# One shared credit for the side work of a two-layer trunk kernel, and a different opening

## The chip, the cores and the metric

The kernel runs on one core of a Trainium2 chip. The metric is the device time of one execution in microseconds (us), the median of several runs. The engines are TensorE (PE in the tables, with its weight loads as PEld), VectorE (DVE), ScalarE (ACT), GpSimd (POOL, almost idle here) and SyncE (SP), whose instruction queue issues most of the DMAs.

## The reference, cut to what matters

Two layers; T = 256 tokens, D = 2048, all in float32.

```python
h   = rms_norm(x, g_pre_mix)
z   = h @ w_in          # one projection, columns split among three head groups
o_h = hgrn2(q, f, i, g) # 6 heads, gated linear recurrence in chunks of 64 tokens
o_s = s5(u)             # 512 channels, 2048 complex diagonal states, scan over T, GELU, half-GLU
o_r = retention(q, k, v, g)  # 6 heads, rotary q/k, chunks of 64 tokens, RMSNorm per head
x   = x + rms_norm((concat(o_h, o_s, o_r) * beta) @ w_out, g_post_mix)
x   = x + rms_norm(conv_gated_ffn(rms_norm(x, g_pre_ffn)), g_post_ffn)   # d_ff = 5632
```

## The kernel before, in words

**Chunks.** All weights pass through one list, `chunks`. A chunk is 128 x 2048 float32 (128 x 1536 for a 384-wide group), moved by SP into one of three `raw` buffers (`dma`, L363). Each chunk is split in two halves: ACT casts a half to the high part `whi` (`split_hi`, L400), and DVE subtracts to give the low part `wlo` (`split_lo` through the helper `tt`, L138). `whi` and `wlo` have four buffers each, so that the halves of two chunks can lie ahead of PE. PE multiplies high by high, high by low and low by high: L424 to L426 where the weights are the stationary operand, L430 to L432 where h is, L437 and L442 where two of the three products are merged into one 512-column matmul.

**The order of the chunks** in a layer (201 of them; the second layer begins with chunk 201): 0 to 3 the input of S5, 4 to 27 the projections that feed HGRN2's and retention's gates, queries and keys (384 wide; 36 matmuls of 256 columns each), 28 to 51 those with h stationary (values and output gates; 24 matmuls of 512 columns), 52 to 59 the first part of `w_out` (merged; 16 matmuls of 512 and 16 of 256 columns), 60 the half-GLU of S5, which needs the end of the scan, 61 to 68 the rest of `w_out`, and then the FFN.

**The side work.** The recurrences are Python generators. HGRN2 (`hg_gen`), retention (`rt_gen`) and the gated outputs stand in the list `side`, called the heads below; S5 (`prep`, `s5_pre`, `s5_gen`) stands in `side5`, called the scan. Each `yield` hands back an estimate of the work issued, in ns. After every chunk the main loop (L1411 to L1426) gives each list a credit of its own, so that a chunk is followed by some 2400 of heads and some 2000 of scan:

```python
for lst, b0, b1 in ((side, 2400, 2400), (side5, 2000, 2200)):
    credit = (b1 if ch.last else b0) + min(0, lst.credit)
```

A generator whose input isn't there yet yields 0 and the list is left. HGRN2's first half can begin after chunk 7, its heads proper after chunk 12, retention after chunk 27. The scan's work per quarter `i` is four reads of PE products into `k` tiles, ten 1024-column products and sums on DVE (L138, `k<-k,k`), four pairs of scans of 256 columns (L705, L707) with three short carry chains of eight 4-column products (L138, `s5p`), and eight matmuls for its output. `head_out` is the end of a head group: products (L747), squares (ACT, L753), a reciprocal root in some ten 6-column steps on DVE (`rsqrt_wide`; tiles `rq`, `hrs`), and a scaling (ACT, L768); `gate_out` transposes (PE, L777) and multiplies (DVE, L141).

**The scheduler.** The program is a list of instructions per engine, in an order that follows issue order and data. Each engine works off its own list in order, so what stands ahead of a `wlo` on DVE delays it.

**The opening.** SP issues the constants, the norm gains (`pks`), then the eight tiles of x (L1337) and the first three chunks in turn; chunk 0 comes in two DMAs. `first_pre` (L1281) transposes x (L1288), and `tile` writes the high part of h on ACT (L247) and the low part on DVE (L251). `feed(-1)` has the first chunk's halves cast whole. `warm` (L222) issues matmuls whose result nobody reads.

Of the kernel before, what the change touches and what calls it, by code (L numbers as in the profile page):

```python
# [9 lines left out]
F32 = mybir.dt.float32  # L10
# [5 lines left out]
MULT, ADD, SUB = ALU.mult, ALU.add, ALU.subtract  # L16

P = 128
T = 256
D = 2048  # L20
# [53 lines left out]
def trunk_kernel(ctx, tc, x, w_in, w_out, w_glu, w_up, w_down, pk, s5bc, cst, glast, out, depth=2):  # L74
    nc = tc.nc
    V, S, PE, G = nc.vector, nc.scalar, nc.tensor, nc.gpsimd
# [19 lines left out]
    def nm(s):  # L96
        cnt[0] += 1
        return f"{s}{cnt[0]}"

    def k4(dt=F32):  # L100
        return kp.tile([P, 1024], dt, tag="k", name=nm("k"))

    def spt():
        return sp.tile([P, 512], F32, tag="sp", name=nm("sp"))
# [9 lines left out]
    ones = const.tile([P, P], F32, name="ones")  # L114
    invd = const.tile([P, 1], F32, name="invd")
# [21 lines left out]
    def tt(out, a, b, op):  # L137
        return V.tensor_tensor(out, a, b, op=op)  # L138
# [83 lines left out]
    def warm(n, lhs, rhs):  # L222

        if n:
            ps = spt()
            m = lhs.shape[-1]
            for _ in range(n):
                PE.matmul(ps[0:m, 0:T], lhsT=lhs, rhs=rhs, start=True, stop=True)

    def pair(t, k):  # L230

# [3 lines left out]
    class Norm:  # L235
# [15 lines left out]
            return V.scalar_tensor_tensor(lo, src, PC(self.l, self.gn, k, k + 1), hi.bitcast(F32), op0=MULT, op1=SUB)  # L251

        def tile(self, g, q, src):
            self.high(4 * g + q, src)
            self.low(4 * g + q, src)

        def group(self, g):
            for q in range(4):
# [108 lines left out]
    def dma(ch, cut=1):  # L367
        g = ch.g
        ch.raw = rawp.tile([P, 2048], F32, tag="raw", name=nm("raw"))
        n = 0  # L370
        ks = ch.ks
        lim = len(ks) // cut
        while n < len(ks):
            m = n + 1
            while m < min(len(ks), n + lim) and ks[m] == ks[m - 1] + 1:
                m += 1
            at = 0
            for c0, w in g.cols:
                nc.sync.dma_start(
                    out=ch.raw[:, n * g.width:m * g.width].rearrange("p (k f) -> p k f", f=g.width)[:, :, at:at + w],  # L380
                    in_=g.w[ks[n] * P:(ks[n] + m - n) * P, c0:c0 + w].rearrange("(k p) f -> p k f", p=P),
                )
                at += w
            n = m

    def split_hi(ch, part):
        g = ch.g
        nk = len(ch.ks)
        h = (nk + 1) // 2
        a, b = (0, h) if part == 0 else (h, nk)  # L390
        if a == b:
            return
        n = (b - a) * g.width
        if ch.early:
            hi, lo = k4(F32R), k4(F32R)
        else:
            hi = wp.tile([P, 1024], F32R, tag="hi", name=nm("whi"))
            lo = wp.tile([P, 1024], F32R, tag="lo", name=nm("wlo"))
        src = ch.raw[:, a * g.width:b * g.width]
        S.copy(out=hi[:, 0:n], in_=src)  # L400
        ch.halves[part] = (hi, lo, src, n)
        for k in range(a, b):
            o = (k - a) * g.width
            ch.parts.append((hi[:, o:o + g.width], lo[:, o:o + g.width]))

    def split_lo(ch, part):
        if part in ch.halves:
            hi, lo, src, n = ch.halves.pop(part)
            tt(lo[:, 0:n], src, hi[:, 0:n].bitcast(F32), SUB)

    def split(ch, part):
        split_hi(ch, part)
        split_lo(ch, part)
# [78 lines left out]
    def matmul(ch):  # L492
        g = ch.g
        if ch.i == 0:
            g.ps = []
            for _ in range(g.nt):
                if g.wide:
                    use_sp = wide[0] % 7 >= 4
                    wide[0] += 1
                    g.ps.append(spt() if use_sp else mp.tile([P, 512], F32, tag="mp", name=nm("mp")))  # L500
                else:
                    g.ps.append(mp.tile([P, 512], F32, tag="mp", name=nm("mp")))
        nk = len(ch.ks)
        if g.merge:
            merged(ch)
        elif ch.last:
            for j in range(g.nt):
                for kk in range(nk):
                    mms(ch, kk, j)
        else:  # L510
            for kk in range(nk):
                for j in range(g.nt):
                    mms(ch, kk, j)
# [420 lines left out]
    class Side(list):  # L934
        credit = 0

    side, side5 = Side(), Side()
    pend = []
    chunks = []
# [326 lines left out]
    def norm_post(nrm, extra, d):  # L1266
        def fp(i):
            def f():
                for g in range(4):
                    if min(3, max(g, d)) == i:  # L1270
                        nrm.sq(g)
                if i == 3:
                    nrm.finish()
                    if extra:
                        extra()
            return f
        return {i: [fp(i)] for i in range(4)}

    xt = []

    def first_pre(n1, extra):  # L1281
        def fg(g):
            def f():
                for q in range(4):
                    ps = spt()
                    for i in range(2):
                        o = ((4 * g + q) % 8) * P
                        PE.transpose(ps[:, i * P:(i + 1) * P], xt[g // 2][i][:, o:o + P], ident)  # L1288
                    n1.tile(g, q, ps[:, 0:T])
                    if g == 0 or q % 2:  # L1290
                        V.tensor_copy(xs[g][:, q, :], ps[:, 0:T])
                    else:
                        S.copy(out=xs[g][:, q, :], in_=ps[:, 0:T])
            return f
        return {g: [fg(g)] for g in range(4)}, norm_post(n1, extra, 2)
# [31 lines left out]

    xf = x.rearrange("b t d -> (b t) d")
    ng = PK["gpre"][1]
    nc.sync.dma_start(out=cs[:, 0:P], in_=cst[:, 0:P])  # L1330
    nc.sync.dma_start(out=pks[:, 0:ng], in_=pk[:, 0:ng])
    for c in range(2):
        xt.append([k4() for _ in range(2)])
    for c in range(4):
        for i in range(2):
            o = (c % 2) * 512
            nc.sync.dma_start(out=xt[c // 2][i][:, o:o + 512], in_=xf[i * P:(i + 1) * P, c * 512:(c + 1) * 512])  # L1337
        if c < 3:
            dma(chunks[c], 2 if c == 0 else 1)
    nc.sync.dma_start(out=pks[:, ng:], in_=pk[:, ng:])  # L1340
    nc.sync.dma_start(out=cs[:, P:NCS], in_=cst[:, P:NCS])
    G.memset(ones, 1.0)
    G.memset(invd, 1.0 / D)

    def prep():
        V.tensor_copy(lmask, C("lmask"))
# [4 lines left out]
    n = len(chunks)  # L1351
    nd = [3, 0]
# [22 lines left out]
    def feed(i):  # L1375
        while nd[1] < n and (nd[1] <= i + 1 or (nd[1] <= i + 4 and all(c.early for c in chunks[i + 2:nd[1] + 1]))):
            while nd[0] < min(n, nd[1] + 3):
                dma(chunks[nd[0]])
                nd[0] += 1
            c = chunks[nd[1]]  # L1380
            if c.mid and nd[1] > i + 1:
                break
            if after and c.hold:
                with tc.issue_after(after[0][0].ins), tc.issue_after(after[0][1].ins):
                    split(c, 0)
                    split(c, 1)
            else:
                split(c, 0)
                split(c, 1)
            c.raw = None  # L1390
            nd[1] += 1

    feed(-1)
    for i, ch in enumerate(chunks):
        for f in ch.g.pre.get(ch.i, []):
            f()
        matmul(ch)
        if ch.g.post_first:
            feed(i)
            for f in ch.g.post.get(ch.i, []):  # L1400
                f()
        if ch.last:
            for j in range(ch.g.nt):
                ch.g.evac(j, ch.g.ps[j])
            ch.g.ps = None
        ch.parts = []
        feed(i)
        if not ch.g.post_first:
            for f in ch.g.post.get(ch.i, []):
                f()  # L1410
        for lst, b0, b1 in ((side, 2400, 2400), (side5, 2000, 2200)):  # L1411
            credit = (b1 if ch.last else b0) + min(0, lst.credit)
            progress = True
            while credit > 0 and lst and progress:
                progress = False
                for gen in list(lst):
                    if credit <= 0:
                        break
                    try:
                        c = next(gen)  # L1420
                        progress = progress or c > 0
                        credit -= c
                    except StopIteration:
                        lst.remove(gen)
                        progress = True
            lst.credit = credit  # L1426
        side.extend(pend)
        pend.clear()
    drain_all()
# [97 lines left out]
```

## Time and profile before

| | |
|---|---|
| median of the runs | 2365.92 us (2364.02 to 2366.3, 3 runs) |
| the profiled execution | 2366.07 us, its span 2364.2 us |
| PE busy | 2329.7 us, 99% of the span, 13740 matmuls |
| DVE busy | 1757.4 us, 74% |
| ACT busy | 1243.4 us, 53% |
| DMA | 418.74 MB, mean 177 GB/s |
| chain that ended last, by engine | PE 92%, DVE 6% |

The profiled execution is 0.15 us above the median. The span is the time from its first to its last instruction; 1.9 us lie around it. A row of the timeline gives start, duration, engine, line, operation, output tile, input tiles and shapes; "x4" at its end means four of the same kind in a row, with the duration over all. What stands in brackets is idle time before it and what ended it. PE's rows overlap, since a matmul's start lies before the end of the one ahead; the distance between starts is what one costs.

### The profile page before, as it was taken

The numbers are of one execution on the slowest core, as the hardware profiler recorded it, in microseconds if no ns is written. First come the engines' busy times: TensorE is split into PE (matmuls) and PEld (weight loads), VectorE is DVE, ScalarE is ACT, GpSimd is POOL, SyncE is SP. The second block draws the span as 40 slices with busy tenths as digits, with TensorE's granted clock in tenths as the row PEclk, the third lists the DMA queues.
The fourth block names the chain that finished last, engine by engine and source line by source line (L and its number), as shares of the span: only waits on it lengthen the run. The fifth ranks groups of instructions, "written<-read, shape, count | busy, mean of one in ns | idle before, by whom it ended". The sixth has DMA issues, their size and how long they took to land.

```text
span 2364.2 us, 34867 instructions
## 1 busy us (share of the span) xinstructions
PE 2329.7 (99%) x13740; PEld 2046.6 (87%) x13740; DVE 1757.4 (74%) x3125; ACT 1243.4 (53%) x1866; POOL 3.5 (0%) x10
## 2 busy tenths in 40 slices
PE   8999999999999999999999999999999999999997
PEld 8998778888888888888989978888888888888886
DVE  7988878977775457776699985879777754677755
ACT  5444655656554445554553446556655544555542
POOL 0000000000000000000000000000000000000000
PEclk9999999999999999999999999999999999999999
DMA  6544445455555555555534444554565565565553
GB/s 232 156 142 161 158 145 191 148 197 189 185 196 195 182 193 180 194 196 186 202 117 147 141 146 152 182 177 167 178 201 192 178 200 193 179 210 183 194 196 125
DMA packets 224468, 418.74 MB, mean 177 GB/s; under 512 B 7344, under 2 KB 48432, under 8 KB 224304
## 3 DMA queue, kind: packets, MB, share of 16 engines
q1 hardware_dynamic: 224016, 415.46, 53.0%
q8 instruction: 108, 1.77, 0.3%
q0 software_dynamic: 288, 1.05, 0.1%
q14 instruction: 56, 0.46, 0.1%
HBM read 414.39 MB, written 2.10 MB: 176 GB/s over the span
## 4 chain that ended last, share of the span: by engine, by line
PE 92%; DVE 6%; issue 1%; ACT 0%; DMA 0%; SPq 0%; DVEq 0%; ACTq 0%
PE mp L437 26%; PE mp L442 13%; PE sp L437 12%; PE mp L430 6%; PE sp L442 6%; PE mp L432 6%; PE mp L431 6%; PE mp L424 4%; PE mp L425 4%; PE mp L426 4%; DVE k L138 2%; DVE wlo L138 2%; PE sp L825 1%; PE sp L660 1%; PE sp L747 1%
## 5 line engine op out<-in xcount | busy, mean ns | idle before, releaser
L138 DVE TENSOR_TENSOR wlo<-raw,whi 128x1024 fp32r<-128x1024 f32 (+1 forms) x792 | 929.2, 1188 | 426.2 <-ACT whi L400 195.3
L400 ACT CAST whi<-raw 128x1024 fp32r<-128x1024 f32 (+1 forms) x792 | 805.0, 1023 | 695.2 <-PE mp L432 214.7
L437 PE MATMUL mp<-h,whi 128*128 128x512 f32 x1576 | 420.9, 390 | 0.9 <-DVE h L251 0.9
L437 PEld LDWEIGHTS mp<-h,whi 128*128 128x128 f32 x1576 | 291.8, 188 | 58.7 <-DVE h L251 1.5
L437 PE MATMUL sp<-h,whi 128*128 128x512 f32 x1176 | 325.9, 390 | 0.9 <-DVE h L251 0.9
L442 PE MATMUL mp<-h,wlo 128*128 128x256 f32 x1576 | 281.2, 283 | 0.0
L437 PEld LDWEIGHTS sp<-h,whi 128*128 128x128 f32 x1176 | 217.8, 188 | 44.0 <-DVE h L251 1.5
L437 PE MATMUL mp<-k,whi 128*128 128x512 f32 x1072 | 254.1, 391 | 0.0
L442 PEld LDWEIGHTS mp<-h,wlo 128*128 128x128 f32 x1576 | 235.9, 191 | 6.2 <-ACT h L247 0.3
L437 PEld LDWEIGHTS mp<-k,whi 128*128 128x128 f32 x1072 | 198.9, 189 | 39.8 <-issue 0.4
L442 PE MATMUL sp<-h,wlo 128*128 128x256 f32 x1176 | 229.6, 283 | 0.0
L138 DVE TENSOR_TENSOR k<-k,k 128x1024 f32<-128x1024 f32 (+9 forms) x244 | 221.0, 929 | 5.6 <-ACT k L267 2.9
L425 PE MATMUL mp<-h,whi 128*128 128x256 f32 x672 | 190.9, 286 | 0.6 <-DVE h L251 0.6
L424 PE MATMUL mp<-h,whi 128*128 128x256 f32 x672 | 190.5, 290 | 0.9 <-ACT whi L400 0.3
L442 PEld LDWEIGHTS sp<-h,wlo 128*128 128x128 f32 x1176 | 185.3, 191 | 4.8 <-ACT h L247 0.3
L426 PE MATMUL mp<-h,wlo 128*128 128x256 f32 x672 | 189.2, 285 | 0.1
L141 DVE SCALAR_TENSOR_TENSOR k<-k,pks,k 128x255 f32<-128x255 f32 (+1 forms) x352 | 163.3, 477 | 0.0
L430 PE MATMUL mp<-whi,h 128*128 128x512 f32 x384 | 153.6, 400 | 0.0
L432 PE MATMUL mp<-whi,h 128*128 128x512 f32 x384 | 150.9, 393 | 0.0
L431 PE MATMUL mp<-wlo,h 128*128 128x512 f32 x384 | 150.1, 391 | 0.0
L442 PEld LDWEIGHTS mp<-k,wlo 128*128 128x128 f32 x1072 | 135.4, 192 | 4.0 <-issue 0.4
L442 PE MATMUL mp<-k,wlo 128*128 128x256 f32 x1072 | 137.5, 284 | 0.0
(230 smaller groups left out, 2955.0 us busy)
## 6 DMA issues: line engine op xcount, KB each, us to landing
raw<-in_w_up_dram SPq DMA_DIRECT2D x176, 1024.0 KB, 5.0
raw<-in_w_down_dram SPq DMA_DIRECT2D x88, 1024.0 KB, 5.0
raw<-in_w_in_dram SPq DMA_DIRECT2D x39, 1024.0 KB, 5.1
raw<-in_w_in_dram SPq DMA_DIRECT2D x48, 768.0 KB, 4.5
raw<-in_w_out_dram SPq DMA_DIRECT2D x24, 1024.0 KB, 5.1
raw<-in_w_in_dram SPq DMA_DIRECT2D x34, 512.0 KB, 4.8
raw<-in_w_out_dram SPq DMA_DIRECT2D x16, 512.0 KB, 4.4
k<-in_x_dram SPq DMA_DIRECT2D x8, 256.0 KB, 7.9
```

Source lines behind the costliest of these rows:

```text
L138: return V.tensor_tensor(out, a, b, op=op)
L141: V.scalar_tensor_tensor(out, a, s, b, op0=op0, op1=op1)
L400: S.copy(out=hi[:, 0:n], in_=src)
L424: PE.matmul(o, lhsT=a, rhs=xhi, start=first, stop=False)
L425: PE.matmul(o, lhsT=a, rhs=xlo, start=False, stop=False)
L426: PE.matmul(o, lhsT=b, rhs=xhi, start=False, stop=last)
L430: PE.matmul(o, lhsT=a, rhs=whi, start=first, stop=False)
L431: PE.matmul(o, lhsT=a, rhs=wlo, start=False, stop=False)
L432: PE.matmul(o, lhsT=b, rhs=whi, start=False, stop=last)
L437: PE.matmul(ch.g.ps[j][:, 0:2 * T], lhsT=a, rhs=ch.g.xop(ch.ks[kk])[2], start=start, stop=stop)
L442: PE.matmul(ch.g.ps[j][:, 0:T], lhsT=b, rhs=ch.g.xop(ch.ks[kk])[0], start=False, stop=False)
L660: PE.matmul(ps[:, w * T:(w + 1) * T], lhsT=Bm[r * 32:(r + 1) * 32, w * 512 + i * P:w * 512 + (i + 1) * P], rhs=u[r * 32:(r + 1) * 32, i * ...
```

## The change

Two parts. First, the two credits become one: after each chunk 4500 (less what the heads overdrew) goes to the heads first, and what they leave, everything while they wait for input, goes to the scan. Second, the opening: the first two tiles of x are issued by ACT's queue, chunk 0 comes in four DMAs and chunk 1 in two; chunk 0's casts and subtractions are made per 512 columns, its second half after the second x tile; PE begins with nine `warm` matmuls on a constant and five more after the second x tile; and of the first four copies of x, two are moved from DVE to ACT.

```diff
@@ def warm
-                PE.matmul(ps[0:m, 0:T], lhsT=lhs, rhs=rhs, start=True, stop=True)
+                PE.matmul(ps[0:m, 0:rhs.shape[-1]], lhsT=lhs, rhs=rhs, start=True, stop=True)
@@
+    def cuts(ch, n):
+
+        w = ch.g.width if ch is chunks[0] else n
+        return [(o, o + w) for o in range(0, n, w)]
...
-        S.copy(out=hi[:, 0:n], in_=src)
+        for o, e in cuts(ch, n):
+            S.copy(out=hi[:, o:e], in_=src[:, o:e])
...
-            tt(lo[:, 0:n], src, hi[:, 0:n].bitcast(F32), SUB)
+            for o, e in cuts(ch, n):
+                tt(lo[:, o:e], src[:, o:e], hi[:, o:e].bitcast(F32), SUB)
@@ def first_pre
-                    n1.tile(g, q, ps[:, 0:T])
-                    if g == 0 or q % 2:
+                    ab = n1.tile(g, q, ps[:, 0:T])
+                    if g == 0 and q < 2:
+                        x0.append(ab[0])
+                        if q:
+                            warm(5, ones, ones)
+                    if q % 2:
@@ the opening's DMAs
+    G.memset(ones, 1.0)
+    G.memset(invd, 1.0 / D)
+    for c in range(2):
+        xt.append([k4() for _ in range(2)])
+    for i in range(2):
+        xdma(nc.scalar, 0, i)
     nc.sync.dma_start(out=cs[:, 0:P], in_=cst[:, 0:P])
     nc.sync.dma_start(out=pks[:, 0:ng], in_=pk[:, 0:ng])
...
-    for c in range(4):
+    dma(chunks[0], 4)
+    for c in range(1, 4):
         for i in range(2):
-            o = (c % 2) * 512
-            nc.sync.dma_start(out=xt[c // 2][i][:, o:o + 512], in_=xf[i * P:(i + 1) * P, c * 512:(c + 1) * 512])
+            xdma(nc.sync, c, i)
         if c < 3:
-            dma(chunks[c], 2 if c == 0 else 1)
+            dma(chunks[c], 2 if c == 1 else 1)
...
+    warm(9, ones, ones)
@@ main loop
+        if i == 0:
+            with tc.issue_after(x0[1].ins):
+                split(ch, 1)
+            ch.raw = None
...
-        for lst, b0, b1 in ((side, 2400, 2400), (side5, 2000, 2200)):
-            credit = (b1 if ch.last else b0) + min(0, lst.credit)
+
+        credit = 4500 + min(0, side.credit)
+        for lst in (side, side5):
             progress = True
...
-            lst.credit = credit
+        side.credit = credit
```

**What it moves, first place: DVE between the last low half of chunk 14 and the first of chunk 15.** `k` tiles of 1024 columns and `s5p` are the scan's, `k` tiles of 384 and 768 columns mostly HGRN2's, `cs` are constants. Before:

```order
L138 TENSOR_TENSOR wlo_1206<-raw_1075,whi_1205 128x768
L138 TENSOR_TENSOR k_958<-k_952,s5p_601 128x512
L138 TENSOR_TENSOR k_951<-k_951,s5p_601 128x16x32
L138 TENSOR_TENSOR k_952<-k_952,s5p_601 128x16x32
L138 TENSOR_TENSOR k_951<-k_951,k_958 128x16x32
L138 TENSOR_TENSOR k_1209<-sp_1145,cs 128x384
L138 TENSOR_TENSOR k_958<-k_951,s5p_601 128x512
L138 TENSOR_TENSOR k_1209<-sp_1149,cs 128x384
L138 TENSOR_TENSOR k_952<-k_952,k_958 128x16x32
L138 TENSOR_TENSOR k_1071<-k_1071,k_804 128x768
L138 TENSOR_TENSOR wlo_1260<-raw_1135,whi_1259 128x768
```

And now:

```order
L138 TENSOR_TENSOR k_1062<-k_1062,s5p_575 128x4
L138 TENSOR_TENSOR k_995<-k_995,s5p_575 128x4
L138 TENSOR_TENSOR k_1317<-sp_1254,cs 128x384
L711 SCALAR_TENSOR_TENSOR k_994<-k_779,k_1062 128x256
L713 SCALAR_TENSOR_TENSOR k_1063<-k_779,k_995 128x256
L138 TENSOR_TENSOR k_1062<-k_994,k_777 128x1024
L138 TENSOR_TENSOR k_995<-k_1063,k_778 128x1024
L138 TENSOR_TENSOR k_994<-k_994,k_778 128x1024
L138 TENSOR_TENSOR k_1062<-k_1062,k_995 128x1024
L138 TENSOR_TENSOR k_1063<-k_1063,k_777 128x1024
L138 TENSOR_TENSOR k_1164<-k_1164,k_907 128x768
L138 TENSOR_TENSOR wlo_1382<-raw_1240,whi_1381 128x768
```

In the changed program 14 rows stand between those two low halves (one of 1024 columns and a few short ones aren't shown), where nine stood; they are the scan's fourth block of a quarter and its closing products, where before the scan was still making its tables of angles (`s5p` operands of 512 columns). The scans, L705 and L707 in the numbering before, are L711 and L713 here. Counted to the second low half of chunk 22, 364 DVE instructions stood ahead before and 414 do now: 18 more of the scan's 1024-column products, 12 more scans of 256 columns, 34 more 4-column products, and some fewer small ones. In the second layer, counted from its beginning to the second low half of its last 384-wide chunk (number 228), it is 16, 14 and 46 more.

**Second place: DVE at the reciprocal root of a `head_out`, near chunk 43.** Before:

```order
L138 TENSOR_TENSOR wlo_2987<-raw_2869,whi_2986 128x1024
L141 SCALAR_TENSOR_TENSOR hrs_2897<-rq_2898,hrs_2897 128x6
L138 TENSOR_TENSOR k_2761<-k_2761,k_2661 128x1024
L138 TENSOR_TENSOR rq_2898<-hrs_2897 128x6
L138 TENSOR_TENSOR wlo_2991<-raw_2869,whi_2990 128x1024
L141 SCALAR_TENSOR_TENSOR rq_2898<-rq_2898,sv_2894 128x6
L138 TENSOR_TENSOR k_2660<-k_2660,k_952 128x1024
L141 SCALAR_TENSOR_TENSOR hrs_2897<-rq_2898,hrs_2897 128x6
L138 TENSOR_TENSOR k_2762<-k_2762,k_951 128x1024
L138 TENSOR_TENSOR hrs_2897<-hrs_2897,cs 128x6
```

And now:

```order
L138 TENSOR_TENSOR rq_3019<-hrs_3018 128x6
L138 TENSOR_TENSOR wlo_3105<-raw_2956,whi_3104 128x1024
L141 SCALAR_TENSOR_TENSOR rq_3019<-rq_3019,sv_3015 128x6
L141 SCALAR_TENSOR_TENSOR hrs_3018<-rq_3019,hrs_3018 128x6
L138 TENSOR_TENSOR rq_3019<-hrs_3018 128x6
L141 SCALAR_TENSOR_TENSOR rq_3019<-rq_3019,sv_3015 128x6
L141 SCALAR_TENSOR_TENSOR hrs_3018<-rq_3019,hrs_3018 128x6
L138 TENSOR_TENSOR hrs_3018<-hrs_3018,cs 128x6
L138 TENSOR_TENSOR wlo_3109<-raw_2956,whi_3108 128x1024
```

The scan's 1024-column products are gone from between the steps of the root: with the shared credit the scan is through after chunk 37 (after chunk 238 in the second layer), where before it took until chunk 59 (254).

**Third place: ACT at the beginning** (`k` tiles are x, `sp` its transposes, row repeats are written x2). Before:

```order
L247 ACT_TABLE_LOAD
L247 ACTIVATE h_131<-sp_128,pks 128x256
L400 CAST whi_120<-raw_103 128x1024
L247 ACTIVATE h_131<-sp_135,pks 128x256
L400 CAST whi_124<-raw_103 128x1024
```

And now:

```order
L1343 DMA k_97<-in_x_dram 128x512
L1343 DMA k_98<-in_x_dram 128x512
L405 ACT_TABLE_LOAD
L405 CAST whi_133<-raw_105 128x512 x2
L247 ACTIVATE h_142<-sp_139,pks 128x256
L247 ACTIVATE h_142<-sp_146,pks 128x256
```

The casts of chunk 0's first half now stand ahead of the first tile of h, and are two of 512 columns.

## Rows read from the trace of the kernel before

**Rows 1.** The page: busy time by engine.

```profile
PE 2329.7 (99%) x13740; PEld 2046.6 (87%) x13740; DVE 1757.4 (74%) x3125; ACT 1243.4 (53%) x1866; POOL 3.5 (0%) x10
```

**Rows 2.** Windows: PE, PEld, DVE, ACT, POOL, PEclk, DMA, GB/s.

```profile
60.00:160.00 100.00, 98.85 (x831) 95.90 (x832) 96.03 (x232) 44.67 (x60) 0.00 (x0) 1.00 0.48 151
345.20:348.50 3.30, 3.24 (x11) 2.86 (x12) 2.31 (x5) 0.48 (x1) 0.00 (x0) 0.50 0.72 224
1410.20:1413.50 3.30, 2.91 (x13) 2.91 (x14) 3.14 (x6) 0.00 (x0) 0.00 (x0) 0.50 0.11 12
```

**Rows 3.** Lines by form, PE alone, from chunk 22's start to chunk 60's.

```profile
L660 PE MATMUL sp<-k,k 32*128 32x256 f32 x48 | 9.0, 400 | 0.0
L825 PE MATMUL sp<-k,k 128*128 128x64 f32 x72 | 8.8, 271 | 0.2 <-DVE k L138 0.2
L747 PE MATMUL sp<-k,k 128*128 128x128 f32 x60 | 8.7, 276 | 2.2 <-ACT k L768 2.2
L777 PE MATMUL sp<-cs,k 128*128 128x128 f32 x24 | 4.1, 289 | 2.1 <-DVE k L141 2.1
L722 PE MATMUL sp<-k,k 128*32 128x256 f32 x32 | 3.2, 391 | 0.0
```

**Rows 4.** The same view of the second layer, chunk 228 to 261.

```profile
L747 PE MATMUL sp<-k,a 128*128 128x128 f32 x12 | 3.2, 361 | 2.8 <-DVE k L138 2.8
```

**Rows 5.** Timeline of ACT: the scaling of a head group.

```profile
276.31 1.66 ACT L768 ACTIVATE k<-sp,hrs 128x128 f32<-128x128 f32 x6 [3.62 <-DVE hrs L138]
```

**Rows 6.** Timeline of SP, ACT and PE at the opening.

```profile
1.65 0.90 SPq L1337 DMA_DIRECT2D k<-in_x_dram  x2
...
7.89 1.04 ACT L400 CAST whi<-raw 128x1024 fp32r<-128x1024 f32 x1 [0.81 <-DMA raw<-in_w_in_dram]
...
8.99 0.58 PE L424 MATMUL mp<-h,whi 128*128 128x256 f32 x1 [0.25 <-ACT whi L400]
13.64 0.41 PE L424 MATMUL mp<-h,whi 128*128 128x256 f32 x1
13.85 0.39 PE L425 MATMUL mp<-h,whi 128*128 128x256 f32 x1
```

**Rows 7.** Timeline of DVE: the scan's three kinds of work.

```profile
128.54 0.68 DVE L705 TENSOR_TENSOR_SCAN k<-k,k 128x256 f32<-128x256 f32 x1
...
129.73 0.36 DVE L138 TENSOR_TENSOR s5p<-s5p,k 128x4 f32<-128x4 f32 x4
...
271.35 1.22 DVE L138 TENSOR_TENSOR k<-k,k 128x1024 f32<-128x1024 f32 x1
272.49 0.16 DVE L138 TENSOR_TENSOR rq<-hrs 128x6 f32<-128x6 f32 x1
```

**Rows 8.** Windows with DVE alone: a layer's beginning to chunks 22 and 228.

```profile
37.60:132.00 94.40, 90.79 (x304) 1.00 0.51 157
1201.90:1336.60 134.70, 125.58 (x275) 1.00 0.48 149
```

**Rows 9.** Timeline of DVE: the second low halves of chunks 22 and 228.

```profile
131.03 0.95 DVE L138 TENSOR_TENSOR wlo<-raw,whi 128x768 fp32r<-128x768 f32 x1
...
1335.61 0.95 DVE L138 TENSOR_TENSOR wlo<-raw,whi 128x768 fp32r<-128x768 f32 x1
```

**Rows 10.** Timeline of PE: first matmuls of chunks 22, 60, 228 and 261.

```profile
134.41 0.28 PE L424 MATMUL mp<-h,whi 128*128 128x256 f32 x1
...
385.85 0.28 PE L424 MATMUL mp<-k,whi 128*128 128x256 f32 x1
...
1341.19 0.36 PE L424 MATMUL mp<-h,whi 128*128 128x256 f32 x1
...
1559.18 0.28 PE L424 MATMUL mp<-k,whi 128*128 128x256 f32 x1
```

**Rows 11.** The chain of waits: two merged runs of 32 matmuls.

```profile
358.83 7.30 PE mp L437 x32
366.13 3.83 PE mp L442 x32
```

More of the change, by code (lines that the diff above doesn't have):

```diff
@@ L253, in tile @@
         def tile(self, g, q, src):
-            self.high(4 * g + q, src)
-            self.low(4 * g + q, src)
+            return self.high(4 * g + q, src), self.low(4 * g + q, src)
         def group(self, g):
@@ L1279, in trunk_kernel @@
     xt = []
+    x0 = []
     def first_pre(n1, extra):
@@ L1329, in trunk_kernel, with xdma @@
     ng = PK["gpre"][1]
+    def xdma(eng, c, i):
+        o = (c % 2) * 512
+        eng.dma_start(out=xt[c // 2][i][:, o:o + 512], in_=xf[i * P:(i + 1) * P, c * 512:(c + 1) * 512])
+    G.memset(ones, 1.0)
[4 more added lines that the diff above has]
+        xdma(nc.scalar, 0, i)
     nc.sync.dma_start(out=cs[:, 0:P], in_=cst[:, 0:P])
     nc.sync.dma_start(out=pks[:, 0:ng], in_=pk[:, 0:ng])
-    for c in range(2):
-        xt.append([k4() for _ in range(2)])
-    for c in range(4):
+    dma(chunks[0], 4)
+    for c in range(1, 4):
         for i in range(2):
-            o = (c % 2) * 512
-            nc.sync.dma_start(out=xt[c // 2][i][:, o:o + 512], in_=xf[i * P:(i + 1) * P, c * 512:(c + 1) * 512])
+            xdma(nc.sync, c, i)
         if c < 3:
-            dma(chunks[c], 2 if c == 0 else 1)
+            dma(chunks[c], 2 if c == 1 else 1)
     nc.sync.dma_start(out=pks[:, ng:], in_=pk[:, ng:])
     nc.sync.dma_start(out=cs[:, P:NCS], in_=cst[:, P:NCS])
-    G.memset(ones, 1.0)
-    G.memset(invd, 1.0 / D)
+    warm(9, ones, ones)
     def prep():
@@ L1388, in feed @@
                 split(c, 0)
+                if c is chunks[0]:
+                    nd[1] += 1
+                    return
                 split(c, 1)
```

## The prediction

> **What bounds the kernel now.** I read the busy times of the page first: PE is busy for 2329.7 us [rows 1], so the change can only win what PE still loses, and it leaves the amount of work on PE and DVE as it is. Then I read the windows by stage, since 74% of DVE is an average. In the first 100 us of the scan DVE is busy for 96.03 of 100 us beside PE's 98.85 [rows 2]: there two engines are full at once, and DVE, which makes the low halves that PE eats, has almost nothing to spare. The lines of PE show the other end of the stage. From chunk 22 to chunk 60 PE stands 2.2 us ahead of `head_out`'s products and 2.1 us ahead of `gate_out`'s transposes, the first waiting for ACT's scaling, the second for DVE [rows 3]; in the second layer it is 2.8 us ahead of retention's products [rows 4]. ACT itself stood 3.62 us, waiting for the last step of a reciprocal root on DVE [rows 5]. After two of these stalls the granted clock is 0.50 for 3.3 us, the 1.2 GHz level [rows 2]. So the scan crowds DVE early and delays the heads late. The change moves scan work from late to early, which relieves the one place and loads the other; the sum decides.
>
> **Part A, the opening.** Before, the first product of the main work starts at 8.99, released by ACT's cast, which begins at 7.89 and takes 1.04 for 1024 columns [rows 6]. Now chunk 0 comes in quarters and x goes out on another queue. But the first casts stand ahead of the first h on ACT, so h still waits for two pieces of weights. I take the first product 1.1 us earlier, about the cast that is no longer waited for whole (-1.1). Its products follow one another at 0.21 us (13.64 to 13.85) [rows 6], where a matmul of 256 columns takes 0.12 later (32 in 3.83) [rows 11]; that is PE at the lower level from 8.99 until 14.06. If the warm matmuls bring the rise ahead, half of those 5.07 us is won: -2.5. Together -3.6, and rounded to -3.5 since five warm matmuls stand between. Bounds: 0 (h waits behind the casts and the clock rises as late as now) and -6.3 (the 1.1 and all of the 5.2 us that chunks 0 to 3 take above their spacing later). The x tiles are issued in 0.90 us for two by SP [rows 6]; now these leave on ACT while SP issues weights.
> The Trainium skill, in "DMA: Bandwidth & Descriptors", section "Issuing engines are not separate DMA queues", says that issuing on several engines saves only the time to initiate, because the transfers share the same 16 DMA engines. By that rule x and weights together land 0.9 us earlier and no more, and the sum below would be 0.2 us higher. No row of before shows two queues at once.
>
> **Part B, DVE falls behind early in the layer.** By the orders, 18 products of 1024 columns, 12 scans and 34 four-column products more stand ahead of chunk 22's second low half. Start to start a product takes 1.14 us (271.35 to 272.49), a scan 0.60 (1.19 for a pair), a four-column product 0.076 (0.28 to 0.36 for four) [rows 7]: 20.5 + 7.2 + 2.6, less 1.8 for the small ones that moved back, is 28.5 us more work. Of it, the idle time of DVE can take 94.40 - 90.79 = 3.6 us [rows 8]. The low half ends at 131.98 [rows 9]; PE, which starts chunk 22 at 134.41 [rows 10] and needs the second half after 18 matmuls of 0.12, at 136.57, leaves a margin of 4.6. So PE is late by 28.5 - 3.6 - 4.6 = **20.3 us**. Until then the two-chunk buffer is empty and each chunk starts as DVE delivers. In the second layer, at chunk 228, it is 16 products (18.2), 14 scans (8.4), 46 small ones (3.5), less 0.3: 29.8; less 134.70 - 125.58 = 9.1 of idle time [rows 8] and a margin from 1336.56 [rows 9] to 1341.19 + 2.16 = 1343.35 [rows 10] of 6.8: **13.9 us**. Together +34.2. Beyond these chunks DVE has less to do than before, since the scan is through twenty chunks sooner, and PE sets the pace again.
>
> **Part C, what comes back behind it.** From chunk 22's start to the half-GLU it is now 385.85 - 134.41 = 251.4 us [rows 10]. What PE must do there in the changed order, by spacing: 6 chunks of 36 matmuls at 0.12 (25.9), 24 of 24 at 0.227 (130.8), 8 of 5.55 (44.4; 16 at 7.30/32 and 16 at 3.83/32 [rows 11]), side work of 34.4: 235.5. That is **-15.9**. Some 6.2 of it is scan work that PE does earlier now (12 of the 24 input matmuls, half of 9.0, and 9 of 32 of the output's 6.2 [rows 3]; PE does it while it waits for DVE in part B), and the rest stalls: 2.2 and 2.1 [rows 3], 1.65 for half of 3.3 us at clock 0.50 [rows 2], some 4 in small gaps. In the second layer, from chunk 228 to 261, 1559.18 - 1341.19 = 218.0 [rows 10] against 4.3 + 130.8 + 44.4 and side work of 27.7, 207.2: **-10.8**, with 2.8 at the score tile [rows 4] and another 1.65 of clock [rows 2]. Together -26.7. The stalls go because in the new order nothing of the scan stands between the steps of a reciprocal root.
>
> **Part D, what the two sums leave out.** B takes DVE as never idle while it lags, and C takes no stall at all. DVE reads what PE and ACT made, and a late PE makes it wait in turn. I have no row for this; the nearest is DVE's idle time now, 3.6 and 9.1 us [rows 8], so I take 2 a layer (0 to 8), and for stalls that stay 1.5 a layer (0 to 3), about two thirds of one of the 2.2 us [rows 3]. That is +7, between 0 and +22.
>
> **Other edits cost nothing.** Two copies of x go from DVE to ACT; both engines have work there, but only of 0.4 us each. The FFN has no side work of the scan beyond what stands in the same places, and its order is unchanged.
>
> **Sum.** 2366.07 (the profiled execution, 0.15 above the median) - 3.5 + 34.2 - 26.7 + 7 = **2377**. This kernel's measurement can tell about 0.2%, 4.7 us, from no change.
>
> **Rivals.**
> 1. Faster: DVE's lag is half of what I count. Much of the added work would fit where DVE waits for a buffer or a PE result inside its busy share, or the half in the buffer reaches further. For it: PE loses only 1.15 us in the 100 us that I call crowded, so no shortage shows there now [rows 2]. Against it: 96.03 of 100 us busy. Then 2366.07 - 3.5 + 17.1 - 26.7 + 4 = 2357. It decides where the lag is below 23.2 us. Chance 0.2.
> 2. Slower by more: bursts. In the new order some 11.6 us of DVE work stand between two low halves (the 14 rows of chunks 14 and 15), and two chunks of 36 matmuls in the buffer last 8.6 us. After a burst PE has run dry; when PE has caught up, DVE cannot run ahead, as `wlo` has four buffers. I count some five such bursts a layer at 1.5 us each beyond the sum: +15, 2392. For it: PE and DVE are both near full. Against it: while DVE lags on average, its buffers are always free, and the bursts lie inside the lag. Chance 0.12.
> 3. No change: lag and recovery cancel (B and C differ by 7.5, and A gives back 3.5), with D near 0: 2370, or less if C recovers the 2 to 4 us that I leave. Chance 0.2.
> 4. The opening doesn't do what it says (the clock rises as late, h waits): 3.5 more than any of these, within the range.
>
> **How the numbers follow.** My forecast, slower by some 11 us through DVE's lag, has 0.48; the rivals 0.2, 0.12 and 0.2. Faster by over 0.2% is rival 1, 0.2; within 0.2% is rival 3, 0.2; slower is the forecast with rival 2, 0.6. The range goes from 2358 (rival 1's upper part) to 2390 (D's bound on the forecast's side, short of rival 2's full price). The forecast's own range, 2371 to 2388, stands beside it, since both signs have a share.
>
> **What would show it.** B: windows of DVE from 60 to 200 near 100% busy; PE rows of chunks 9 to 28 with gaps released by `wlo`; chunk 28's first matmul 15 to 20 us late, and in the second layer 10 to 14 us more. C: the idle times ahead of L747 and L777's counterparts, and the stretches at clock 0.50 in 345 and 1410, gone. A: first main product near 7.9, with spacing 0.12 from the start. I am wrong if PE's starts of chunk 28 are within 5 us of before (rival 1), or if the late stalls stay although the scan ended earlier.

## The result and the profile after

The changed kernel takes 2401.23 us (median of 4 runs, 2399.13 to 2407.93), the kernel before 2365.16 in the same session: a ratio of 1.0158, 95% interval 1.0146 to 1.0170. It is slower by 36 us, where 11 were forecast and 24 was the upper end of the range. The medians below are over all executions of a kernel; of scan_cap2000's five one took 4673.90 us, which its ratio leaves out, and the median of the other four is 2374.31.

The page of the changed kernel: PE is busy 20 us longer than before [rows 1], in a span that is 36 us longer, and the chain that ended last runs through DVE for 11%, before for 6%.

```profile
PE 2349.7 (98%) x13768; PEld 2058.4 (86%) x13768; DVE 1759.1 (73%) x3125; ACT 1244.5 (52%) x1870; POOL 3.5 (0%) x10
...
PE 87%; DVE 11%; issue 1%; ACT 1%; DMA 0%; DVEq 0%; SPq 0%; ACTq 0%
```

Line numbers in the rows of the changed kernel are six higher than before in most of what follows (its L430 is L424 before, L666 is L660); ACT's cast, L400 before, is L405.

Where the time went is read from windows that end at the same chunk in both kernels. The columns are PE, PEld, DVE, ACT, POOL, then clock, DMA share and GB/s. The kernel before, from chunk 4 to 22, to 34, to 60 in the first layer, and from 205 to 228, to 233, to 261 in the second:

```profile
39.86:134.41 94.55, 93.60 (x783) 91.89 (x782) 91.48 (x305) 46.22 (x64) 0.00 (x0) 1.00 0.51 157
134.41:213.22 78.81, 78.60 (x525) 69.55 (x523) 71.35 (x123) 30.13 (x39) 0.00 (x0) 1.00 0.46 148
213.22:385.85 172.63, 168.33 (x874) 137.92 (x873) 135.98 (x297) 97.77 (x203) 0.00 (x0) 0.99 0.49 161
1211.88:1341.19 129.31, 128.19 (x1055) 122.84 (x1053) 122.68 (x281) 57.43 (x82) 0.00 (x0) 1.00 0.48 150
1341.19:1376.52 35.33, 35.33 (x207) 29.08 (x206) 33.42 (x57) 11.96 (x13) 0.00 (x0) 1.00 0.46 146
1376.52:1559.18 182.66, 179.63 (x920) 148.00 (x919) 133.52 (x246) 100.13 (x205) 0.00 (x0) 0.99 0.50 161
```

The same six stretches of the changed kernel:

```profile
36.90:154.55 117.65, 105.21 (x824) 98.11 (x822) 115.05 (x344) 49.88 (x74) 0.00 (x0) 0.97 0.39 120
154.55:240.46 85.91, 84.86 (x554) 72.24 (x553) 79.13 (x149) 31.95 (x47) 0.00 (x0) 1.00 0.47 151
240.46:398.32 157.86, 156.10 (x801) 131.34 (x800) 106.11 (x235) 89.96 (x183) 0.00 (x0) 1.00 0.53 172
1224.39:1373.92 149.53, 137.65 (x1063) 127.53 (x1061) 140.72 (x330) 62.16 (x92) 0.00 (x0) 0.95 0.38 119
1373.92:1426.17 52.25, 49.07 (x264) 38.23 (x263) 36.61 (x56) 16.94 (x25) 0.00 (x0) 0.97 0.42 132
1426.17:1595.00 168.83, 168.14 (x854) 141.06 (x853) 112.83 (x197) 93.09 (x184) 0.00 (x0) 1.00 0.53 174
```

Chunk 4 begins at 36.90 in place of 39.86: the opening gave 3.0 us. Then the first layer loses 23.1 us up to chunk 22 (117.65 against 94.55), 7.1 more up to chunk 34, and gets 14.8 back. The second loses 20.2 up to chunk 228, 16.9 in the five chunks behind it, and gets 13.8 back. -3.0 + 23.1 + 7.1 - 14.8 + 20.2 + 16.9 - 13.8 = 35.7, of 36.2 by which the spans differ. The FFNs between take the same time.

PE's side of it, from the same rows: in the six stretches together it stands idle for 31.0 us, where it was 9.6, and it is busy for 701.0 us, where it was 683.7, with about as many matmuls. In each layer it has more matmuls in the first two stretches and fewer in the third: part of what is lost early and given back late is PE's own work on the scan, which now stands earlier.

The waits show who makes PE late. Of PE in the stretch 30 to 200, by what it waited for (us in total, times, longest), in the changed kernel:

```profile
PE mp L432 <- DVE wlo L138: 8.4, 4, 5.4
PE sp L728 <- DVE k L138: 1.6, 1, 1.6
```

and before, where in this stretch no matmul of the main work waits for a `wlo`:

```profile
PE sp L613 <- DVE k L138: 0.6, 1, 0.6
PE sp L825 <- DVE k L138: 0.6, 2, 0.4
```

In the timeline of the changed kernel the longest of these waits ends at 82.32, and behind it the matmuls of 256 columns follow one another at 0.22 us where they took 0.12 ahead of it:

```profile
76.59 0.28 PE L431 MATMUL mp<-h,whi 128*128 128x256 f32 x1
...
82.32 0.58 PE L432 MATMUL mp<-h,wlo 128*128 128x256 f32 x1 [5.45 <-DVE wlo L138]
82.70 0.42 PE L430 MATMUL mp<-h,whi 128*128 128x256 f32 x1
82.92 0.42 PE L431 MATMUL mp<-h,whi 128*128 128x256 f32 x1
```

The windows of the changed kernel around and behind such waits have the clock at its 1.2 GHz level, in the first layer once and in the second four times:

```profile
80.20:86.80 6.60, 4.48 (x21) 4.48 (x22) 6.60 (x9) 0.00 (x0) 0.00 (x0) 0.50 0.36 113
...
1254.40:1257.70 3.30, 3.30 (x17) 3.30 (x17) 3.30 (x7) 1.45 (x2) 0.00 (x0) 0.50 0.55 154
1285.10:1288.40 3.30, 3.30 (x21) 1.94 (x20) 2.30 (x3) 1.74 (x3) 0.00 (x0) 0.50 0.73 238
1329.50:1336.20 6.70, 6.17 (x33) 5.83 (x34) 6.70 (x10) 1.34 (x3) 0.00 (x0) 0.50 0.40 119
1380.70:1384.00 3.30, 3.30 (x19) 3.30 (x17) 3.30 (x7) 0.00 (x0) 0.00 (x0) 0.50 0.70 203
```

What stood in the way at 82.32, in chunk 11, is plain in DVE's timeline: the scan's last steps for its tables of angles and the first 1024-column products of a quarter, and then the low half that PE needed.

```profile
77.81 1.22 DVE L138 TENSOR_TENSOR k<-k,k 128x1024 f32<-128x1024 f32 x1
78.96 0.17 DVE L138 TENSOR_TENSOR s5p<-s5p 128x16 f32<-128x16 f32 x1
79.04 2.35 DVE L138 TENSOR_TENSOR k<-k,k 128x1024 f32<-128x1024 f32 x2
81.31 1.82 DVE L138 TENSOR_TENSOR wlo<-raw,whi 128x768 fp32r<-128x768 f32 x2
```

### The profile page after: what moved, and what is told of

It is laid out like the page before. It is cut to its first block, busy times and chain, and to the rows that moved or that the text cites. A ratio compares the mean times of both kernels' runs of the same rounds, so it can differ in the third digit from the quotient of the medians.

```text
span 2400.4 us, 34923 instructions
## 1 busy us (share of the span) xinstructions
PE 2349.7 (98%) x13768; PEld 2058.4 (86%) x13768; DVE 1759.1 (73%) x3125; ACT 1244.5 (52%) x1870; POOL 3.5 (0%) x10
## 4 chain that ended last, share of the span: by engine, by line
PE 87%; DVE 11%; issue 1%; ACT 1%; DMA 0%; DVEq 0%; SPq 0%; ACTq 0%
PE mp L443 26%; PE mp L448 13%; PE sp L443 11%; PE mp L436 6%; PE mp L438 6%; PE mp L437 6%; PE sp L448 6%; DVE k L138 5%; PE mp L432 3%; PE mp L431 3%; PE mp L430 2%; DVE wlo L138 2%; PE sp L831 1%; DVE k L711 1%; PE sp L666 1%
## 5 line engine op out<-in xcount | busy, mean ns | idle before, releaser
L138 DVE TENSOR_TENSOR wlo<-raw,whi 128x1024 fp32r<-128x1024 f32 (+2 forms) x794 | 929.4, 1185 | 461.3 <-ACT whi L405 224.9
L405 ACT CAST whi<-raw 128x1024 fp32r<-128x1024 f32 (+2 forms) x794 | 805.7, 1021 | 719.1 <-PE mp L438 214.7
L448 PEld LDWEIGHTS mp<-h,wlo 128*128 128x128 f32 x1576 | 235.9, 191 | 6.2 <-ACT h L247 0.3
L138 DVE TENSOR_TENSOR k<-k,k 128x1024 f32<-128x1024 f32 (+8 forms) x244 | 219.3, 928 | 6.2 <-ACT k L266 2.4
L430 PE MATMUL mp<-h,whi 128*128 128x256 f32 x672 | 189.6, 291 | 4.7 <-DVE k L138 3.9
L432 PEld LDWEIGHTS mp<-h,wlo 128*128 128x128 f32 x672 | 129.5, 196 | 20.1 <-DVE wlo L138 17.8
```

What stands on the lines that cost most here:

```text
L405: S.copy(out=hi[:, o:e], in_=src[:, o:e])
L430: PE.matmul(o, lhsT=a, rhs=xhi, start=first, stop=False)
L432: PE.matmul(o, lhsT=b, rhs=xhi, start=False, stop=last)
L448: PE.matmul(ch.g.ps[j][:, 0:T], lhsT=b, rhs=ch.g.xop(ch.ks[kk])[0], start=False, stop=False)
```

## The experiments

All runs, against the kernel before on the same chip:

| kernel | median us | ratio to before, 95% interval |
|---|---|---|
| opening alone (opening_only) | 2363.60 | 0.9995 (0.9986 to 1.0005) |
| credit alone (credits_only) | 2405.78 | 1.0171 (1.0154 to 1.0188) |
| scan at most 2000 (scan_cap2000) | 2374.88 | 1.0040 (1.0026 to 1.0055) |
| the same, overdraft kept (scan_cap_debt) | 2372.15 | 1.0035 (1.0022 to 1.0048) |
| shared credit 3600 (credit3600) | 2380.07 | 1.0064 (1.0049 to 1.0079) |
| surplus early alone (open_early) | 2388.62 | 1.0106 (1.0087 to 1.0124) |
| changed, less DVE work (after_less) | 2379.20 | 1.0065 (1.0050 to 1.0080) |
| before, less DVE work (before_less) | 2360.10 | 0.9980 (0.9971 to 0.9990) |
| pause of one chunk (open_hold1) | 2365.90 | 1.0006 (0.9996 to 1.0015) |
| pause of eight chunks (open_gap) | 2374.12 | 1.0041 (1.0027 to 1.0056) |
| scan 1500 early, 2600 late (open_late) | 2361.36 | 0.9986 (0.9977 to 0.9995) |
| scan 2300 from chunk 13 (open_2300) | 2367.31 | 1.0011 (1.0001 to 1.0020) |

**Which part it is.** The two parts of the change apart: opening_only has the old loop over two credits in the changed kernel, credits_only the new loop in the old one.

> The new opening with the old separate credits (2400 for the heads, 2000 for the scan). If the time was lost by the shared credit alone (theory: the scan's DVE work, moved ahead of chunk 34 of each layer, makes PE wait), this is before less the 3.0 us that chunk 4 came earlier in the changed kernel: 2362.2, between 2361 and 2364. Rival, the opening or its order costs later what it wins at first: 2366 or more.

> The shared credit with the old opening. Theory: all of the loss and none of the gain, 2401.2 + 3.0 = 2404, between 2400 and 2408. Rival, the two parts work on one another (an earlier start makes the early shortage worse): under 2398.

The loss is the shared credit's: 41.6 us by itself. The opening alone can't be told from no change by its times, though its trace has the 3 us (chunk 4 at 36.5, the span 2361.5 against 2364.2); they fit into the interval, which reaches to 0.9986, or -3.3 us.

**What about the credit.** Three edits of it, the first two by one idea. scan_cap2000 keeps 4500 and the heads' precedence and caps the scan:

```diff
         for lst in (side, side5):
+            if lst is side5:
+                credit = min(credit, 2000)
```

> The changed kernel with one line more: of the shared 4500, heads still first, the scan gets at most 2000 after a chunk, as it did before. Theory (it is the surplus of 4500 for the scan while the heads wait that crowds DVE): 2362 to 2368, the scan ends near chunk 59 again. Rival (heads ahead of the scan, or an overdraft carried over, is what costs): 2385 or more. Second rival (lost clock after gaps, whoever causes them): between, near 2380.

It gave back 26 of 36 us and no more, 2374.88. In this loop, as in the changed kernel, an overdraft of the scan too (not only of the heads) counts against the next 4500 and not against the scan's 2000, so that it still gets more than before. The next kernel mends that:

```diff
+            if lst is side5:
+                side.credit = credit
+                credit = min(max(credit, 0), 2000) + min(0, side5.credit)
...
-        side.credit = credit
+        side5.credit = credit
```

> As scan_cap2000, but what the scan overdraws after one chunk is taken from its own next 2000 (there it was forgiven, so that the scan came to some 3000 a chunk). Theory: now the scan really has its old share, heads still go first out of one 4500, and the rest of the loss goes: 2362 to 2367. Rival (the heads' precedence itself costs the 11 us that were left): 2372 or more.

At 2372.15 it misses its number and meets the rival's, 2372 or more. The trace tells where. Where the changed kernel lost 23 us in the first layer it now loses nothing; its stretch from chunk 4 to chunk 22 is as long as that of opening_only, and as full on both engines (opening_only first):

```profile
36.50:131.00 94.50, 93.64 (x783) 91.93 (x782) 91.43 (x304) 46.20 (x64) 0.00 (x0) 1.00 0.49 158
```

```profile
37.20:131.70 94.50, 93.65 (x783) 91.94 (x782) 91.44 (x304) 46.19 (x64) 0.00 (x0) 1.00 0.49 158
```

What is left comes later. From chunk 22 to 34 it is 3.5 us behind opening_only (82.27 us against 78.80). And the scan, which the heads now hold back further on, isn't through when chunk 60 needs it: PE waits there for the copy of its result, the high part that the half-GLU multiplies (ACT, L737), as the timeline of scan_cap_debt shows.

```profile
386.52 0.74 PE L430 MATMUL mp<-k,whi 128*128 128x256 f32 x4 [2.65 <-ACT k L737]
```

So neither the one credit nor the heads' precedence costs anything ahead of chunk 22; the scan's greater share does. The heads' precedence and their greater share (up to 4500 after a chunk, where it was 2400) cost the rest, later on, 8.6 us against opening_only by the medians; which of the two isn't told apart.

**How much, and when.** credit3600 has 3600 in place of 4500. open_early has the old separate credits, and for the scan 4500 after the first 13 chunks of a layer alone:

```diff
...
+            if lst is side5:
+                j = i % 201
+                b0 = b1 = 4500 if j < 13 else 2000
```

> The changed kernel with a shared credit of 3600 in place of 4500, so that the scan gets 3600 while the heads wait and about 1900 beside them. Theory: the lag follows the DVE work put ahead, which shrinks by about two thirds of what the surplus over 2000 shrinks (1600 against 2500), so two thirds of the loss of 39 us stays at most: 2375 to 2390. Rival (heads first is the cause, whatever the size): 2395 to 2405.

> The new opening, the old separate credits with the heads' 2400 and the scan's 2000, but 4500 for the scan after the first 13 chunks of a layer, where the heads have little or nothing to do. It isolates the surplus that the shared credit gives the scan while the heads wait. Theory (this surplus is what DVE cannot take): 2385 to 2400, PE waiting for low halves in chunks 4 to 22 as in the changed kernel, and the scan through near chunk 47. Rival (what it gets beside the heads and by overdrafts that are forgiven is as bad): 2368 to 2380.

Both as the theory had it: against opening_only, whose scan gets 2000, the loss is 16 us at 3600 and 38 at 4500, and open_early, where the scan gets more only while the heads wait, loses 25. PE again waits for the low halves, the longest time in chunk 11 as in the changed kernel; the view of PE's waits of open_early, from 36 to 200:

```profile
PE mp L432 <- DVE wlo L138: 5.5, 2, 4.4
```

**Is it DVE's work?** after_less and before_less leave out the four sums and differences among the scan's 1024-column products and sums per quarter on DVE (twelve in the program, not the ten that I counted ahead of the prediction), and nothing else:

```diff
-            tt(a, a, b_, ADD)
...
-            tt(xi, xi, xr, SUB)
...
-            tt(a, a, xi, SUB)
...
-            tt(b_, b_, xr, ADD)
```

> The changed kernel without four of the scan's ten 1024-column sums and differences per quarter on DVE (the scan's result is not S5's; PE, ACT and the DMAs do the same as before): 16 fewer a layer, 18.2 us of DVE work by 1.14 us each, most of it ahead of chunk 34. Theory (PE waits for DVE as a whole, so that a us taken from DVE there is nearly a us of time): 2365 to 2375. Rival (the loss is in gaps for other reasons: scan input on PE, ACT blocked, clock): 2388 to 2400.

> The kernel before without the same 16 products a layer. Theory: DVE is near full here too but PE lost only 3 us ahead of chunk 34, so little can be won: 2356 to 2364, the stalls behind chunk 34 a little shorter. Rival (DVE already sets the pace before the change): 2345 or less.

The same 36.5 us of DVE work (32 by 1.14; by the pages DVE is busy 33.6 and 32.9 us less) are worth 22.0 us in the changed kernel and 4.1 in the one before. So DVE's work sets the pace in the one and hardly in the other. It was worth less than I had expected, by 4 us or more, and after_less, which has 36.5 us less to do on DVE than the kernel before, still takes 15.0 us more: what the rest of the moved work does there isn't split further. The wait in chunk 11 stays (4.3 of 5.4 us), since only one of the products in front of it was left out.

**Can the late stalls be had for less?** The stalls of part C are real, so I tried to take them away without the early loss. open_hold1 gives the scan nothing after the chunk in which a `head_out` begins its root, and 2600 from chunk 28 on; open_gap gives it nothing after chunks 36 to 43, 2300 before them from chunk 28 on, and 3000 after:

```diff
...
+                b0 = b1 = 2000 if j < 28 else 2300 if j < 36 else 0 if j < 44 else 3000
```

> The new opening, the old credits, and no scan credit after the chunk in which a head_out begins its reciprocal root; from chunk 28 of a layer the scan gets 2600 in place of 2000 to make up for it. Theory (in the kernel before, the scan's 1.14 us products between the root's steps cause PE's late stalls of 2 to 3 us and the clock's fall after them): 2354 to 2360. Rival (these stalls only move to the next wait): 2362 to 2367.

> The new opening, the old credits, and no scan credit at all after chunks 36 to 43 of a layer, where the four head groups end, with 2300 before (28 to 35) and 3000 after them. Theory (the late stalls come from scan products that the engine has ahead of or between the root's steps, which one chunk's pause did not take away because they had been issued before): the stalls at the ends of the head groups go, 2353 to 2360. Rival (they move to the scan's end, which now is hurried and due at chunk 60): 2362 to 2370.

Both failed. In open_hold1 the stall ahead of `head_out`'s products is still there (2.32 us at 275.5): products that were issued earlier stand between the root's steps as before. In open_gap it is gone in the first layer, and the scan's end is late instead:

```profile
386.83 1.23 PE L430 MATMUL mp<-k,whi 128*128 128x256 f32 x4 [4.60 <-ACT k L737]
```

**The other direction.** open_late moves scan work from early to late, open_2300 a little of it to the front (the same line, with 1500 if j < 28 else 2600, and 2000 if j < 13 else 2300).

> The new opening, separate credits, the scan getting 1500 in place of 2000 after the first 28 chunks of a layer and 2600 after them: the opposite of the change, scan work moved from early to late. Theory (the old 2000 already sits just below what DVE can take early, PE losing only some 3 us a layer there, so there is little to win early; and more scan late means more of it among the ends of the head groups and nearer its due time): 2364 to 2375. Rival (DVE limits PE early in the kernel before too, and relief there is a gain): 2357 or less.

> The new opening, separate credits, 2000 for the scan after the first 13 chunks as before and 2300 after them: a small step of the scan towards the front, through by chunk 55. Theory (DVE has no slack beside the heads ahead of chunk 34 either, the little that moves is lost there and partly won late): 2363 to 2371. Rival (a little earlier is better, the change merely overdid it): 2360 or less, a version that beats both.

open_2300 went as the theory had it. open_late, at 2361.36, came out between the theory (2364 or more) and the rival (2357 or less); it is the fastest kernel here that leaves nothing out, 2.6 us under the one before, with an interval that leaves out 1 by little. How much of that is its opening isn't told apart, as opening_only's interval overlaps with it. In its trace PE is busy 99.79 us of the 100 us from 60 to 160, before 98.85 [rows 2]:

```profile
60.00:160.00 100.00, 99.79 (x844) 98.58 (x843) 93.07 (x228) 41.48 (x56) 0.00 (x0) 1.00 0.49 157
```

## Why the prediction was wrong

**What held.** The direction, and the reason for it: DVE falls behind early. Part B's count of the moved work came out within 0.5 us. The rows are windows with DVE alone, from the start of chunk 4's first low half to the start of the second low half of chunk 22 and of chunk 228, before and in the changed kernel:

```profile
35.02:131.03 96.01, 92.40 (x307) 1.00 0.52 162
1204.27:1335.61 131.34, 122.22 (x270) 1.00 0.48 151
```

```profile
32.06:155.32 123.26, 120.50 (x355) 0.97 0.40 126
1216.78:1379.59 162.81, 151.49 (x346) 0.96 0.39 122
```

DVE is busy 28.1 and 29.3 us longer, where the count had 28.5 and 29.8. Chunk 28 begins 17.8 us late (192.03 against 174.27), where 15 to 20 were forecast. Part A had -3.5, and it was -3.0: the first product starts at 8.07 (I had 7.9), and 256 columns take 0.12 us from 9.04 on, 5 us sooner than before [rows 6].

```profile
8.07 0.74 PE L430 MATMUL mp<-h,whi 128*128 128x256 f32 x4 [0.17 <-ACT h L247]
8.82 0.38 PE L431 MATMUL mp<-h,whi 128*128 128x256 f32 x1
9.04 0.28 PE L432 MATMUL mp<-h,wlo 128*128 128x256 f32 x1
9.16 0.28 PE L431 MATMUL mp<-h,whi 128*128 128x256 f32 x1
```

Whether the second issuing queue is worth more than the time to issue can't be decided by the 0.2 us that the two readings differ by. The stalls ahead of the heads' products [rows 3, 4] are gone, with the clock's falls behind them, as C had it: the last stretch of each layer has a clock of 1.00 where it was 0.99.

**The step that failed** is part C's sum first, and then the idle time in part B's. C is defined from chunk 22 to 60 and from 228 to 261. Over these chunks, before and in the changed kernel:

```profile
134.41:385.85 251.44, 246.93 (x1396) 207.46 (x1395) 207.33 (x419) 127.90 (x241) 0.00 (x0) 0.99 0.48 157
1341.19:1559.18 217.99, 214.96 (x1124) 177.08 (x1124) 166.94 (x302) 112.08 (x217) 0.00 (x0) 0.99 0.49 159
```

```profile
154.55:398.32 243.77, 240.96 (x1354) 203.58 (x1353) 185.24 (x383) 121.90 (x230) 0.00 (x0) 1.00 0.51 165
1373.92:1595.00 221.08, 217.21 (x1117) 179.29 (x1115) 149.44 (x252) 110.03 (x208) 0.00 (x0) 0.99 0.50 164
```

C had -15.9 and -10.8, and it was -7.7 and +3.1: 22.1 us of the miss. B had 20.3 and 13.9, and it was 23.1 and 20.2: 9.1 more. With A's 0.5, and less the 7 that D had set aside, that is 24.7 of the 25 us by which the profiled execution, 2402.17, lies above 2377.

In C, PE's busy time alone, 240.96 and 217.21, is above the whole sums, 235.5 and 207.2, which took every matmul at its bare spacing. In the first layer the moved work came out: 42 matmuls fewer and 6.0 us less busy time, where C had 6.2. The other 9.7 us were to be stalls and gaps that go. PE's idle time there was 4.5 us and still is 2.8, since other waits have taken the old ones' place. The rest was never a stall: PE's busy time was some 5 us above C's terms before (246.93 against 235.5 and 6.2), and it still is (240.96 against 235.5). In the second layer PE has 7 matmuls fewer, is busy 2.3 us longer, and is idle for 3.9 us in place of 3.0. The prediction gives no terms for its side work of 34.4 and 27.7 us, so how much of the second layer's miss lies in the latter stays open.

In B the idle time of DVE was to take 3.6 and 9.1 us. By the rows with DVE alone it took 0.9 (3.6 before, 2.8 now) and nothing at all in the second layer (9.1 before, 11.3 now). It was no room: DVE was waiting for what PE and ACT make. Its waits in the second layer's stretch come to 5.6 us for PE and 5.3 for ACT, where they were 1.0 and 7.2. Part D had 2 us a layer for that, up to 8; in the second layer 11.3 us stood idle against 2 in the forecast.

The sentence behind B's sums, "Beyond these chunks DVE has less to do than before, since the scan is through twenty chunks sooner, and PE sets the pace again", is wrong in its first half up to chunk 34. From chunk 22 to 34 DVE has 79.13 us to do, where it had 71.35. But PE does set the pace there: it is busy for 84.86 of 85.91 us at a clock of 1.00, with 29 more matmuls than before. Of the 7.1 us that the changed kernel loses in this stretch 6.3 are PE's busy time, in the main work that PE is spared behind chunk 34, where it has 73 matmuls fewer and 14.8 us come back. It is the same in the second layer's five chunks behind 228: 57 more matmuls there, 66 fewer behind them.

**The second layer** was mis-sized most, and one more thing wasn't in the sum: the clock. I had counted its falls as something that the change takes away late, not as something that new waits bring early. In the five windows with a clock of 0.50 above, PE is busy for 20.6 us (4.48, 3.30, 3.30, 6.17 and 3.30), in the two before for 6.2 [rows 2]. If half of that is lost, which is an estimate, the clock's part of the 36 us is some 7.

DVE's own waits in that layer include a chain over three engines. The timeline of DVE, and of ACT ahead of it:

```profile
1425.17 1.22 DVE L138 TENSOR_TENSOR wlo<-raw,whi 128x1024 fp32r<-128x1024 f32 x1 [9.66 <-ACT whi L405]
```

```profile
1416.85 0.65 ACT L672 COPY k<-sp 128x256 f32<-128x256 f32 x2 [2.22 <-PE sp L666]
1419.03 0.65 ACT L672 COPY k<-sp 128x256 f32<-128x256 f32 x2 [1.53 <-PE sp L666]
...
1423.39 0.65 ACT L672 COPY k<-sp 128x256 f32<-128x256 f32 x2 [1.53 <-PE sp L666]
1424.10 1.05 ACT L405 CAST whi<-raw 128x1024 fp32r<-128x1024 f32 x1
```

The scan's input products (L666) stand on PE in fours between main matmuls; ACT copies each four as they come, and the cast of the next weights stands behind the last copy. DVE, late in the layer, could have caught up in these 9.66 us. PE was not idle then; what it had to do had been moved there.

**The rivals.** The second, bursts, came nearest by its number (2392, at 0.12), and its price of five bursts a layer at 1.5 us is near PE's waits for low halves: four of 8.4 us in the first layer, and in the second six of 5.1 us up to chunk 228 and one of 1.8 behind it.

```profile
PE mp L432 <- DVE wlo L138: 5.1, 6, 1.5
```

Whether these lie beyond the lag or are the lag isn't told apart. The burst that the rival names, between the low halves of chunks 14 and 15, brought no such wait: its six 1024-column products and one of 768 run from 99.19 to 106.85, and PE, which had waited 1.55 us at 103.93 for the scan's result, begins its next matmul on a low half at 109.65 without a wait. What I held against the rival, that the bursts lie inside the lag, fails for the second layer, where DVE was late and idle by turns. The first rival, half the lag, and the third, no change, are excluded by the lag at chunk 22, 23.1 us, and by credits_only; the fourth by part A. That the loss needs the clock isn't shown by an experiment, only read from the windows.

## What to carry to other kernels

When work is moved to an earlier place on an engine that feeds the bound engine, the moved work can be counted from the orders; here that count was right within 0.5 us. What went wrong is what was set against it. Take the feeding engine's idle time for waits until its rows show that it is room. Don't take a later stretch at the bound engine's bare spacing: compare its busy time there with the spacing first, and count as a gain only the idle time whose cause goes. Beside the lag, count the clock: behind a wait the bound engine can be slower too. In this kernel the shared credit became safe early on once the scan's part was capped at what it had before, overdrafts included.

## What the runs showed of the hardware that was not expected

After a wait of 5.45 us PE's matmuls took 0.22 us in place of 0.12 until the clock came back; the granted clock was 0.50 from about 80.2 to 86.8, so it fell while PE still stood and stayed low behind the wait. In the second layer the clock fell behind shorter waits. Those ahead of its four falls, in PE's timeline:

```profile
1253.86 0.65 PE L432 MATMUL mp<-h,wlo 128*128 128x256 f32 x3 [1.54 <-DVE wlo L138]
...
1282.67 0.59 PE L728 MATMUL sp<-k,k 128*32 128x256 f32 x2 [2.06 <-DVE k L138]
...
1328.50 0.39 PE L430 MATMUL mp<-h,whi 128*128 128x256 f32 x1 [1.08 <-DVE k L138]
...
1379.74 0.39 PE L432 MATMUL mp<-h,wlo 128*128 128x256 f32 x1 [1.79 <-DVE wlo L138]
```

Not each such wait brought one: behind the 1.55 us at 103.93 and the 0.99 us at 141.42 the clock stayed at 1.00.

At the opening it is the reverse. After 28 unread matmuls (14 calls, two rows each) and the first transposes the products ran at 0.12 us almost from the first, where before they took 0.21 for five us. The granted clock doesn't show it: from 9.00 to 14.00 it reads 1.00 in both kernels, so there only the spacing tells. That the unread matmuls did it wasn't tested by itself.
